# A hybrid decoder trunk: order of products and readings in the expert dispatch and in the last down projection

## Chip, cores and metric

The kernel runs on one NeuronCore of one Trainium2 chip. The metric is device time in microseconds of one launch, from the first to the last instruction of the core with what lies around it. Engines are named as the profile names them: PE (TensorE matmul), PEld (its weight loads), DVE (VectorE), ACT (ScalarE), POOL (GpSimd), and SP, whose queue issues the large DMA transfers.

## What is computed

One layer (`DEPTH = 1`) on 256 tokens and 16 meta tokens of width 2048: a mixer (an mLSTM branch and a sparse attention branch, gated and summed), a LayerNorm, a two-level mixture of experts, a second LayerNorm. The change lies in the mixture of experts and in what feeds the last LayerNorm:

```python
# 32 experts in 4 groups: best group, then the best 2 experts in it
xb = x2[toks]                                   # tokens routed to expert e
gu = xb @ w_gate_up[e]                          # 2048 x 1024 weights
hb = jax.nn.silu(gu[:, :D_FF]) * gu[:, D_FF:]
ys = (hb @ w_down[e]) * ws[:, None]             # 512 x 2048 weights
ffn = segment_sum(ys, row_tok)                  # back to the tokens
h = layer_norm(ALPHA * h + ffn, ln2_g, ln2_b)   # the output, meta rows dropped
```

All 32 experts are computed, each for the (up to 64) tokens that are routed to it, so all weights of w_gate_up and w_down (402 MB) are read from HBM.

## The kernel before

The mixer fills about the first 785 us. Then the experts run in 16 pairs p (two experts of 64 slots each make 128 rows), and every four experts share one dispatch q (q = 0 to 7, before p = 0, 2, 4, ...).

**Dispatch** (`dispatch`, L1017, `bank`, L1029). One-hot matrices `oh` gather the tokens of four experts: `xe[:, k]` (128 features x 256 slots) is a product of the normed activations, split into a high and a low part `uh` and `ul`, with `oh`. A bank is one PSUM tile `pxe` of 512 columns, which holds two values of k: each half is four products (`uh` and `ul` for both blocks of 128 tokens) into one accumulator of 256 columns. Its first half (k even) is read by DVE (L1050), its second half (k odd) by ACT (L1047), both into `xe`. Tiles `pxe` come from a pool of two (`pd`), so a bank's products also wait for the readings of the bank two before it. A dispatch is 8 banks. In dispatch 0 the first two banks run ahead of all, and then chunk n of the first expert (8 products `gu`, which read `xe` of bank n) alternates with bank n + 2. The other dispatches run their 8 banks one behind the other, between two pairs.

**Up and down.** Pair p has 16 chunks (`up_chunk`, L1120), each of which consumes one transfer of 1 MB (`weg`). Between the chunks stand steps of the previous pair's down projection (`down_step`, L1148; 2 transfers `wed` of 1 MB for every four chunks), and the combinations of its pieces (`combine`, L1254). SP issues all transfers in the fixed order of `specs` (L787 to L803): into a slot as soon as its last product on PE has run (`issue`, L809, `used`, L829). Ahead of every fourth chunk the order has two `wed`. All transfers are in this one queue.

**The last down projection** (L1341) has no later chunks to hide in. It runs in five pieces of columns, `LASTP` = 512, 512, 512, 256, 256, each with its own two transfers `wel`. A piece is 16 products `py` on PE, then `gated` (L1271): ACT scales `py` into a high part `yh` (L1277), DVE makes the low part `yl` from `py` and `yh` (L1278); then `combine`: for each of two token blocks PE multiplies `yh` and `yl` by the one-hot matrix into `pc` (pool `pd` again), DVE adds `pc` to `acc` (L1265), takes its statistics by `bn_stats` (L1250), and POOL multiplies it by a LayerNorm row into `fin` (L1251). The final LayerNorm starts with DVE's `bn_aggr` (L1436), which needs the statistics of all pieces.

The order of PE's instructions is that of the program text (`mm` keeps it); on the other engines a scheduler orders the instructions, and each engine runs its own in order.

Of the kernel before, what the change touches and what calls it, by code (L numbers as in the profile page):

```python
# [48 lines left out]
def trunk(ctx, tc, x, meta, ln_emb_g, ln_emb_b, rel_bias, w_in, conv_w, conv_b, b_ig, b_fg,  # L49
# [190 lines left out]
    def fgroup(c0, name, t0=0, raw0=None):  # L240

        n = L - t0
        nk = 8
        pts = [pmt(f"{name}_p{i}") for i in range(2)]
        for kc in range(KD // nk):
            raw = raw0 if raw0 and not kc else load_w(w_in, kc * nk, nk, c0, 256,
                                                      f"{name}_r{kc}")
            if raw0 and kc:
                small_loads()
            for hf in range(2):  # L250
                if raw0:
                    k = kc * nk + hf * 4
                    for k in range(k + 2 if k else 0, min(k + 6, KD)):
                        embed(k)
                wh, wl = split_w(raw[:, hf * 4:hf * 4 + 4], f"{name}_{kc}{hf}")
                k0 = kc * nk + hf * 4
                for kk in range(4):
                    k = k0 + kk
                    for i in range(2):
                        for r in (xhk, xlk):  # L260
                            nc.tensor.matmul(pts[i][:, :n], lhsT=wh[:, kk, i * P:i * P + P],
                                             rhs=r(k, slice(t0, L)), start=k == 0 and r is xhk,
                                             stop=False)
                for kk in range(4):
                    k = k0 + kk
                    for i in range(2):
                        nc.tensor.matmul(pts[i][:, :n], lhsT=wl[:, kk, i * P:i * P + P],
                                         rhs=xhk(k, slice(t0, L)), start=False, stop=k == KD - 1)
                step()
        return pts  # L270
# [349 lines left out]
    for j in range(AH // 2):  # L620
# [8 lines left out]
        pv = fgroup(O_AV + j * 256, f"av{j}")  # L629
# [159 lines left out]
    for p in range(NE // 2):  # L789
        for n in range(16):  # L790
# [5 lines left out]
            e, kc = 2 * p + n // 8, n % 8  # L796
# [206 lines left out]
    def pdt(name):  # L1003
        return pdp.tile([P, 512], F32, name=name, tag="pd")

    def mm(*a, **k):
        late(nc.tensor.matmul(*a, **k))  # L1007
# [4 lines left out]
    def rows_of(k):  # L1012

        o = (k // 2) * 256 + k % 2
        return slice(o, o + 255, 2)

    def dispatch(q):  # L1017


        oh = me.tile([P, 2, 4, C], F32R, name=f"oh{q}", tag="oh", bufs=1)  # L1020
        for b in R2:
            nc.vector.tensor_tensor(
                oh[:, b], iota[:, None, :C].to_broadcast([P, 4, C]),
                rk[:, b, q * 4:q * 4 + 4].unsqueeze(2).to_broadcast([P, 4, C]),
                op=ALU.is_equal)
        xe = me.tile([P, KD, 4 * C], F32, name=f"xe{q}", tag="xe", bufs=1)
        ohf = oh.rearrange("p b e c -> p b (e c)")

        def bank(kc):  # L1029
            if q == 0 and kc % 2 == 0:  # L1030
                for b in R2:
                    sl = slice(kc * 256, kc * 256 + 512)
                    if kc == 0:
                        nc.gpsimd.tensor_tensor(ul[:, b, sl], u[b][:, sl],
                                                uh[:, b, sl].bitcast(F32), op=ALU.subtract)
                    else:
                        late(nc.vector.tensor_tensor(ul[:, b, sl], u[b][:, sl],
                                                     uh[:, b, sl].bitcast(F32), op=ALU.subtract))
            pt = pdt(f"pxe{q}_{kc}")
            for k in (2 * kc, 2 * kc + 1):  # L1040
                pv = pt[:, k % 2 * 256:k % 2 * 256 + 256]
                for i, part in enumerate((uh, ul)):
                    for b in R2:
                        mm(pv, lhsT=part[:, b, rows_of(k)], rhs=ohf[:, b],
                           start=i == 0 and b == 0, stop=i == 1 and b == 1)
                if k % 2:
                    nc.scalar.activation(xe[:, k], pv, AF.Identity, bias=gbp[:, 1, k:k + 1],  # L1047
                                         scale=gbp[:, 0, k:k + 1])
                else:
                    nc.vector.tensor_scalar(xe[:, k], pv, gbp[:, 0, k:k + 1],  # L1050
                                            gbp[:, 1, k:k + 1], op0=ALU.mult, op1=ALU.add)

        for kc in range(2 if q == 0 else 8):
            bank(kc)
        return xe, ohf, bank
# [198 lines left out]
    def combine(nn, c0, n, yh, yl, ohT, first, last):  # L1254

        for b in R2:
            pc = pdt(f"pc{nn}{b}")
            for i, y in enumerate((yh, yl)):
                mm(pc[:, :n], lhsT=ohT[:, b * P:b * P + P], rhs=y[:, :n],
                                 start=i == 0, stop=i == 1)  # L1260
            av = acc[:, b, c0:c0 + n]
            if first:
                nc.vector.tensor_copy(av, pc[:, :n])
            else:
                nc.vector.tensor_tensor(av, pc[:, :n], av, op=ALU.add)  # L1265
            if last:
                finish(b, c0, n)

    def gated_of(p, cur):

        def gated(c0, n, py):  # L1271
            j = p % 2
            gate = cur[1][:, j:j + 1]
            nn = f"{p}_{c0}"
            yh = pre.tile([P, 512], F32R, name=f"yh{nn}", tag="yh", bufs=2)
            yl = pre.tile([P, 512], F32R, name=f"yl{nn}", tag="yl", bufs=2)
            nc.scalar.activation(yh[:, :n], py[:, :n], AF.Copy, scale=gate)  # L1277
            nc.vector.scalar_tensor_tensor(yl[:, :n], py[:, :n], gate, yh[:, :n].bitcast(F32),  # L1278
                                           op0=ALU.mult, op1=ALU.subtract)
            return lambda: combine(nn, c0, n, yh, yl, cur[0][:, j], p == 0, p == LAST)  # L1280
        return gated

    turn = []
    for p in range(NE // 2):
# [4 lines left out]
        for n in range(16):  # L1289
            e, kc = e0 + n // 8, n % 8  # L1290
# [47 lines left out]
    nm5 = me.tile([P, 2, 4, 32], F32, name="nm5", tag="hb", bufs=1)  # L1338
    nc.vector.memset(nm5, 1.0)
    gated = gated_of(LAST, cur)  # L1340
    for c0, n in LASTP:  # L1341
        py = pyp.tile([P, 512], F32, name=f"py{LAST}_{c0}", tag="py")
        for kk in range(4):
            for i in range(2):
                mm(py[i * 64:i * 64 + 64, :n], lhsT=hTs[LAST][:, kk, 64 - i * 64:128 - i * 64],
                                 rhs=live["l", NE - 2 + i, c0][:, kk], start=kk == 0, stop=kk == 3)
        gated(c0, n, py)()

    mp_ctx.close()

# [12 lines left out]
    with tc.If(nmax > C):  # L1363
        with tc.For_i(0, NE, 1) as e:
# [4 lines left out]
            for part in range(2):  # L1369
# [10 lines left out]
                pt = op.tile([P, 512], F32, name="opt" + nn, tag="o0")  # L1380
# [13 lines left out]
                for kc in range(8):  # L1394
# [3 lines left out]
                    for kk in range(2):  # L1398
                        k = kc * 2 + kk
# [6 lines left out]
                pt = op.tile([P, 512], F32, name="opth" + nn, tag="o0")  # L1406
# [3 lines left out]
                for c in range(4):  # L1410
# [3 lines left out]
                    py = op.tile([P, 512], F32, name=f"opy{c}" + nn, tag="og0")  # L1414
# [36 lines left out]
    for u_, (b, n) in enumerate((b, n) for n in range(4) for b in range(2)):  # L1451
        sl = slice(n * 512, n * 512 + 512)
        r = slice(32 * n, 32 * n + 5)
        pt = fp.tile([P, 512], F32, name=f"pt{u_}", tag="pt", bufs=4)
# [38 lines left out]
```

## Time and profile before

| | us |
|---|---|
| median of 3 runs | 1781.91 (1778.19 to 1784.15) |
| profiled execution, its own time | 1773.8 |
| its span | 1772.1 |
| PE busy | 1648.9 (93%) |
| DVE busy | 707.9 (40%) |
| ACT busy | 457.5 (26%) |
| DMA: bytes, mean rate | 537.06 MB, 303 GB/s |

The profile's times are from the start of the span. The busy shares are means over stages with different limits; the table by stage in the section on rows (Rows 1) divides them: there a line is a stretch, with the busy time of PE, PEld, DVE, ACT and POOL and the number of their instructions, then the granted clock of TensorE as a share of 2.4 GHz, the share of time in which the 16 DMA engines worked, and GB/s. In a timeline a row is one instruction or a merged run of equal ones (x8); the time of a PE row includes how long its last result takes to come out, so that rows overlap, and the pace is read from start to start.

### The profile page before, as it was taken

The numbers are of one execution on the slowest core, as the hardware profiler recorded it, in microseconds if no ns is written. First come the engines' busy times: TensorE is split into PE (matmuls) and PEld (weight loads), VectorE is DVE, ScalarE is ACT, GpSimd is POOL, SyncE is SP. The second block draws the span as 40 slices with busy tenths as digits, with TensorE's granted clock in tenths as the row PEclk, the third lists the DMA queues.
The fourth block names the chain that finished last, engine by engine and source line by source line (L and its number), as shares of the span: only waits on it lengthen the run. The fifth ranks groups of instructions, "written<-read, shape, count | busy, mean of one in ns | idle before, by whom it ended". The sixth has DMA issues, their size and how long they took to land. (4 is left out here: it accounts for less than half of the span.)

```text
span 1772.1 us, 20945 instructions
## 1 busy us (share of the span) xinstructions
PE 1648.9 (93%) x8488; PEld 1013.8 (57%) x8488; DVE 707.9 (40%) x1178; ACT 457.5 (26%) x695; POOL 118.2 (7%) x143
## 2 busy tenths in 40 slices
PE   8999999999999999989989899899897988988986
PEld 7988899988787787873343433432433334324332
DVE  7666754454646556452223323421212123202224
ACT  5343444444443443341110100110111001101111
POOL 3002000000302102000100000000000000000002
PEclk9999999999999999999999999999999999999998
DMA  7534454456565578648999999999999999999993
GB/s 221 169 108 132 144 167 143 143 190 229 179 204 178 167 260 301 222 165 303 418 419 420 419 420 419 420 420 419 420 419 419 419 420 420 419 420 419 420 409 118
DMA packets 155941, 537.06 MB, mean 303 GB/s; under 512 B 15724, under 2 KB 64076, under 8 KB 107824
## 3 DMA queue, kind: packets, MB, share of 16 engines
q1 hardware_dynamic: 153552, 530.54, 77.8%
q0 software_dynamic: 2224, 5.12, 1.0%
q8 instruction: 68, 1.11, 0.3%
q14 instruction: 33, 0.27, 0.0%
q10 hardware_dynamic: 64, 0.02, 0.0%
HBM read 533.53 MB, written 2.11 MB: 302 GB/s over the span
## 5 line engine op out<-in xcount | busy, mean ns | idle before, releaser
L1007 PE MATMUL gu<-weg,xe 128*64 128x512 f32 x2032 | 495.5, 610 | 30.5 <-DMA weg<-in_w_gate_up_dram 30.4
L1007 PEld LDWEIGHTS gu<-weg,xe 128*64 128x64 f32 x2032 | 140.2, 139 | 312.0 <-issue 246.9
L1007 PE MATMUL py<-wed,hT 128*64 128x512 f32 x960 | 246.4, 597 | 0.0
L1007 PEld LDWEIGHTS py<-wed,hT 128*64 128x64 f32 x960 | 69.6, 139 | 140.1 <-issue 138.7
L1277 ACT ACTIVATE yh<-py,gsl 128x512 fp32r<-128x512 f32 (+1 forms) x65 | 44.2, 681 | 355.3 <-PE py L1007 340.7
L1278 DVE SCALAR_TENSOR_TENSOR yl<-py,gsl,yh 128x512 fp32r<-128x512 f32 (+1 forms) x65 | 48.0, 738 | 194.4 <-ACT yh L1277 194.4
L1137 DVE TENSOR_TENSOR hb<-gu,hb 64x512 f32<-64x512 f32 x32 | 22.0, 689 | 243.7 <-ACT hb L1136 243.6
L1265 DVE TENSOR_TENSOR acc<-pc,acc 128x512 f32<-128x512 f32 (+1 forms) x122 | 78.9, 678 | 88.1 <-PE pc L1007 87.3
L1136 ACT ACTIVATE hb<-gu 64x512 f32<-64x512 f32 x32 | 18.9, 591 | 341.6 <-PE gu L1007 341.6
L1007 PE MATMUL pxe<-oh,uh 128*128 128x256 f32 x256 | 61.1, 321 | 46.1 <-DVE xe L1050 42.7
L1007 PEld LDWEIGHTS pxe<-oh,uh 128*128 128x128 f32 x256 | 40.9, 199 | 67.8 <-DVE xe L1050 55.8
L1251 POOL TENSOR_TENSOR fin<-acc,fin 128x512 f32<-128x512 f32 (+1 forms) x10 | 10.3, 1053 | 895.0 <-DVE acc L1265 895.0
L1050 DVE TENSOR_SCALAR xe<-pxe,gbp 128x256 f32<-128x256 f32 x64 | 34.7, 543 | 83.8 <-PE pxe L1007 83.8
L1007 PE MATMUL pc<-yh,ohT 128*128 128x512 f32 (+1 forms) x130 | 59.8, 460 | 6.0 <-ACT yh L1277 3.5
L1047 ACT ACTIVATE xe<-pxe,gbp 128x256 f32<-128x256 f32 x64 | 36.0, 563 | 101.1 <-PE pxe L1007 101.1
L1007 PEld LDWEIGHTS pc<-yh,ohT 128*128 128x128 f32 x130 | 24.7, 190 | 54.9 <-issue 23.8
L1007 PE MATMUL pc<-yl,ohT 128*128 128x512 f32 (+1 forms) x130 | 52.4, 403 | 1.1 <-DVE yl L1278 0.9
L1007 PE MATMUL pxe<-oh,ul 128*128 128x256 f32 x256 | 52.4, 287 | 0.0
L1068 DVE TENSOR_SCALAR ohT<-prk,slot 128x512 fp32r<-128x512 f32 x8 | 6.0, 751 | 93.7 <-PE prk L1007 93.7
L1007 PEld LDWEIGHTS pxe<-oh,ul 128*128 128x128 f32 x256 | 41.4, 201 | 0.0
L1007 PEld LDWEIGHTS pc<-yl,ohT 128*128 128x128 f32 x130 | 25.0, 193 | 4.6 <-DVE yl L1278 2.5
L760 POOL TENSOR_TENSOR gms<-gms,gas 128x512 f32<-128x512 f32 x8 | 10.9, 1389 | 224.0 <-DVE gas L759 224.0
(924 smaller groups left out, 3036.7 us busy)
## 6 DMA issues: line engine op xcount, KB each, us to landing
weg<-in_w_gate_up_dram SPq DMA_DIRECT2D x253, 1024.0 KB, 19.9
wed<-in_w_down_dram SPq DMA_DIRECT2D x120, 1024.0 KB, 19.9
gm_r<-in_w_in_dram SPq DMA_DIRECT2D x16, 1024.0 KB, 5.0
ga_r<-in_w_in_dram SPq DMA_DIRECT2D x16, 1024.0 KB, 5.1
wo_r<-in_w_out_dram SPq DMA_DIRECT2D x16, 1024.0 KB, 5.4
qk_r<-in_w_in_dram SPq DMA_DIRECT2D x8, 1024.0 KB, 5.7
mv_r<-in_w_in_dram SPq DMA_DIRECT2D x8, 1024.0 KB, 5.3
aq_r<-in_w_in_dram SPq DMA_DIRECT2D x8, 1024.0 KB, 5.2
```

The costliest lines, as they stand in the source:

```text
L760: nc.gpsimd.tensor_tensor(sg[0][:, b], sg[0][:, b], sg[1][:, b], op=ALU.add)
L1007: late(nc.tensor.matmul(*a, **k))
L1047: nc.scalar.activation(xe[:, k], pv, AF.Identity, bias=gbp[:, 1, k:k + 1], scale=gbp[:, 0, k:k + 1])
L1050: nc.vector.tensor_scalar(xe[:, k], pv, gbp[:, 0, k:k + 1], gbp[:, 1, k:k + 1], op0=ALU.mult, op1=ALU.add)
L1068: nc.vector.tensor_scalar(ohT.rearrange("p a b -> p (a b)"), pr, slot, None, op0=ALU.is_equal)
L1136: nc.scalar.activation(hb[mine], pg_[other], AF.Silu)
L1137: nc.vector.tensor_tensor(hb[mine], pg_[mine], hb[mine], op=ALU.mult)
L1251: nc.gpsimd.tensor_tensor(fin[1 + b][:, c0:c0 + n], acc[:, b, c0:c0 + n], fin[0][:, c0:c0 + n], op=ALU.mult)
L1265: nc.vector.tensor_tensor(av, pc[:, :n], av, op=ALU.add)
L1277: nc.scalar.activation(yh[:, :n], py[:, :n], AF.Copy, scale=gate)
L1278: nc.vector.scalar_tensor_tensor(yl[:, :n], py[:, :n], gate, yh[:, :n].bitcast(F32), op0=ALU.mult, op1=ALU.subtract)
```

## The change

In `bank` the loop over the two halves is split: first the eight products of both halves, then DVE's reading of the first half and ACT's of the second. In the last down projection the combination of a piece is issued behind the products of the next piece; the last piece's combination follows at the end.

```diff
@@ bank (L1041) @@
             for k in (2 * kc, 2 * kc + 1):
                 pv = pt[:, k % 2 * 256:k % 2 * 256 + 256]
                 for i, part in enumerate((uh, ul)):
                     for b in R2:
                         mm(pv, lhsT=part[:, b, rows_of(k)], rhs=ohf[:, b],
                            start=i == 0 and b == 0, stop=i == 1 and b == 1)
+            for k in (2 * kc, 2 * kc + 1):
+                pv = pt[:, k % 2 * 256:k % 2 * 256 + 256]
                 if k % 2:
                     nc.scalar.activation(xe[:, k], pv, AF.Identity, bias=gbp[:, 1, k:k + 1],
                                          scale=gbp[:, 0, k:k + 1])
                 else:
                     nc.vector.tensor_scalar(xe[:, k], pv, gbp[:, 0, k:k + 1],
                                             gbp[:, 1, k:k + 1], op0=ALU.mult, op1=ALU.add)
@@ last down projection (L1340) @@
     gated = gated_of(LAST, cur)
+    then = None
     for c0, n in LASTP:
...
-        gated(c0, n, py)()
+        nxt = gated(c0, n, py)
+        if then:
+            then()
+        then = nxt
+    then()
```

Three places in the built programs show what moves. The first is PE in a bank of dispatch 1 (`pxe_2` is its third bank; what stands in brackets is the engine whose progress an instruction waits for). Before:

```order
L1007 MATMUL pxe_2_7492<-oh_7466,uh 128x256 [waits Activation_49]
L1007 MATMUL pxe_2_7492<-oh_7466,uh 128x256
L1007 MATMUL pxe_2_7492<-oh_7466,ul 128x256 x2
L1007 MATMUL pxe_2_7492<-oh_7466,uh 128x256 [waits DVE_49]
L1007 MATMUL pxe_2_7492<-oh_7466,uh 128x256
L1007 MATMUL pxe_2_7492<-oh_7466,ul 128x256 x2
L1007 MATMUL pxe_3_7503<-oh_7466,uh 128x256 [waits Activation_49]
```

And with the change:

```order
L1007 MATMUL pxe_2_7492<-oh_7466,uh 128x256 [waits Activation_49]
L1007 MATMUL pxe_2_7492<-oh_7466,uh 128x256
L1007 MATMUL pxe_2_7492<-oh_7466,ul 128x256 x2
L1007 MATMUL pxe_2_7492<-oh_7466,uh 128x256 x2
L1007 MATMUL pxe_2_7492<-oh_7466,ul 128x256 x2
L1007 MATMUL pxe_3_7503<-oh_7466,uh 128x256 [waits Activation_49]
```

The products and their order are the same. The wait for DVE ahead of the second half is gone (it is gone from all 64 banks); the wait for ACT ahead of the bank, which guards the reuse of the tile, stays. ACT's reading waits for DVE's in both programs.

The second place is PE between two pieces of the last down projection (`py_0`, `py_512`, `py_1024` are the products of the pieces that begin at these columns, `pc_00` and `pc_01` the combination of the first piece for the two token blocks). Before:

```order
L1007 MATMUL py_0_11275<-wel_0_11115,hT_11229 64x512
L1007 MATMUL py_0_11275<-wel_0_11117,hT_11229 64x512
L1007 MATMUL pc_00_11288<-yh_0_11284,ohT_11142 128x512
L1007 MATMUL pc_00_11288<-yl_0_11285,ohT_11142 128x512
L1007 MATMUL pc_01_11295<-yh_0_11284,ohT_11142 128x512
L1007 MATMUL pc_01_11295<-yl_0_11285,ohT_11142 128x512
L1007 MATMUL py_512_11302<-wel_512_11119,hT_11229 64x512
L1007 MATMUL py_512_11302<-wel_512_11127,hT_11229 64x512
```

And with the change, where the rows ahead are those of the second piece:

```order
L1007 MATMUL py_512_11288<-wel_512_11119,hT_11229 64x512
L1007 MATMUL py_512_11288<-wel_512_11127,hT_11229 64x512
L1007 MATMUL pc_00_11301<-yh_0_11284,ohT_11142 128x512
L1007 MATMUL pc_00_11301<-yl_0_11285,ohT_11142 128x512
L1007 MATMUL pc_01_11308<-yh_0_11284,ohT_11142 128x512
L1007 MATMUL pc_01_11308<-yl_0_11285,ohT_11142 128x512
L1007 MATMUL py_1024_11315<-wel_1024_11135,hT_11229 64x512
L1007 MATMUL py_1024_11315<-wel_1024_11158,hT_11229 64x512
```

The four products of a combination have moved behind the eight pairs of products of the next piece. The last piece's combination stands behind that of the piece before it.

The third place is DVE in the same stretch, from the first piece's `yl` on. Before:

```order
L1278 SCALAR_TENSOR_TENSOR yl_0_11285<-py_0_11275,gsl_11149,yh_0_11284 128x512
L1265 TENSOR_TENSOR acc<-pc_00_11288,acc 128x512
L1265 TENSOR_TENSOR acc<-pc_01_11295,acc 128x512
L1250 BN_STATS st_7031<-acc 128x6 x4
L1278 SCALAR_TENSOR_TENSOR yl_512_11312<-py_512_11302,gsl_11149,yh_512_11311 128x512
L1265 TENSOR_TENSOR acc<-pc_5120_11315,acc 128x512
L1265 TENSOR_TENSOR acc<-pc_5121_11322,acc 128x512
L1250 BN_STATS st_7031<-acc 128x6 x4
```

And with the change:

```order
L1280 SCALAR_TENSOR_TENSOR yl_0_11285<-py_0_11275,gsl_11149,yh_0_11284 128x512
L1267 TENSOR_TENSOR acc<-pc_00_11301,acc 128x512
L1280 SCALAR_TENSOR_TENSOR yl_512_11298<-py_512_11288,gsl_11149,yh_512_11297 128x512
L1252 BN_STATS st_7031<-acc 128x6 x2
L1267 TENSOR_TENSOR acc<-pc_01_11308,acc 128x512
L1252 BN_STATS st_7031<-acc 128x6 x2
L1267 TENSOR_TENSOR acc<-pc_5120_11328,acc 128x512
L1280 SCALAR_TENSOR_TENSOR yl_1024_11325<-py_1024_11315,gsl_11149,yh_1024_11324 128x512
L1252 BN_STATS st_7031<-acc 128x6 x2
L1267 TENSOR_TENSOR acc<-pc_5121_11335,acc 128x512
L1267 TENSOR_TENSOR acc<-pc_10240_11355,acc 128x512
L1252 BN_STATS st_7031<-acc 128x6 x2
```

Before, a piece's `yl`, its two additions and its four statistics stand together. Now a `yl` of the next piece stands between the two additions of a piece, and the statistics are spread in pairs; further on the second addition of the third piece stands behind the fourth piece's `yl` and two pairs of statistics. The number of instructions is the same (5 `yl`, 10 additions, 16 statistics).

On the other engines the order is as before, but for one exchange in dispatch 1: ACT's `yh` of a pair's last piece and DVE's `gr` now stand ahead of the reading of the dispatch's first bank. SP's and POOL's order is unchanged.

## Rows read from the trace of the kernel before

**Rows 1.** Busy time by engine, granted clock, DMA share and GB/s, by stage.
```profile
790.60:799.60 9.00, 7.65 (x24) 4.41 (x24) 2.39 (x5) 6.41 (x14) 0.00 (x0) 0.50 0.00 0
799.60:821.70 22.10, 18.27 (x92) 9.14 (x92) 7.19 (x19) 2.81 (x5) 0.00 (x0) 1.00 0.82 301
...
860.00:1709.00 849.00, 770.59 (x3522) 301.05 (x3518) 200.39 (x340) 95.29 (x155) 0.00 (x0) 0.98 1.01 420
...
1730.00:1757.00 27.00, 20.87 (x100) 8.42 (x100) 13.85 (x31) 3.59 (x6) 10.07 (x10) 1.00 0.25 84
```

**Rows 2.** Timeline of PE, first dispatch: start us, length us, instruction, [idle before, releaser].
```profile
790.60 0.80 PE L1007 MATMUL pxe<-oh,uh 128*128 128x256 f32 x2 [1.19 <-ACT u L948]
791.20 0.63 PE L1007 MATMUL pxe<-oh,ul 128*128 128x256 f32 x2
...
793.56 0.63 PE L1007 MATMUL pxe<-oh,uh 128*128 128x256 f32 x2
793.99 0.63 PE L1007 MATMUL pxe<-oh,ul 128*128 128x256 f32 x2
...
796.40 3.50 PE L1007 MATMUL gu<-weg,xe 128*64 128x512 f32 x8
799.84 0.52 PE L1007 MATMUL pxe<-oh,uh 128*128 128x256 f32 x2
...
801.23 0.51 PE L1007 MATMUL pxe<-oh,uh 128*128 128x256 f32 x2 [0.64 <-DVE xe L1050]
...
801.91 1.94 PE L1007 MATMUL gu<-weg,xe 128*64 128x512 f32 x8
```

**Rows 3.** Timeline of SP's DMA issues, 785 to 835 us.
```profile
830.47 3.76 SPq L823 DMA_DIRECT2D weg<-in_w_gate_up_dram  x3
```

**Rows 4.** The page's costliest groups: the two readings of the banks.
```profile
L1050 DVE TENSOR_SCALAR xe<-pxe,gbp 128x256 f32<-128x256 f32 x64 | 34.7, 543 | 83.8 <-PE pxe L1007 83.8
...
L1047 ACT ACTIVATE xe<-pxe,gbp 128x256 f32<-128x256 f32 x64 | 36.0, 563 | 101.1 <-PE pxe L1007 101.1
```

**Rows 5.** Timeline of PE inside dispatch 7.
```profile
1606.03 0.40 PE L1007 MATMUL pxe<-oh,uh 128*128 128x256 f32 x2
1606.27 0.40 PE L1007 MATMUL pxe<-oh,ul 128*128 128x256 f32 x2
```

**Rows 6.** Timeline of PE: chunks that waited for a weight transfer.
```profile
1212.86 3.49 PE L1007 MATMUL gu<-weg,xe 128*64 128x512 f32 x8 [2.48 <-DMA weg<-in_w_gate_up_dram]
...
1694.77 3.68 PE L1007 MATMUL gu<-weg,xe 128*64 128x512 f32 x8 [4.44 <-DMA weg<-in_w_gate_up_dram]
...
1709.73 1.94 PE L1007 MATMUL gu<-weg,xe 128*64 128x512 f32 x8 [0.51 <-DMA weg<-in_w_gate_up_dram]
```

**Rows 7.** Timeline of PE in the closing stretch.
```profile
1717.61 0.50 PE L1007 MATMUL pc<-yh,ohT 128*128 128x512 f32 x1
...
1718.73 1.94 PE L1007 MATMUL gu<-weg,xe 128*64 128x512 f32 x8
...
1729.90 3.65 PE L1007 MATMUL py<-wel,hT 128*64 128x512 f32 x16
...
1736.02 3.65 PE L1007 MATMUL py<-wel,hT 128*64 128x512 f32 x16
```

**Rows 8.** Timeline of DVE in the closing stretch.
```profile
1734.32 0.75 DVE L1278 SCALAR_TENSOR_TENSOR yl<-py,gsl,yh 128x512 fp32r<-128x512 f32 x1 [5.26 <-ACT yh L1277]
1735.66 1.29 DVE L1265 TENSOR_TENSOR acc<-pc,acc 128x512 f32<-128x512 f32 x2 [0.59 <-PE pc L1007]
1736.87 1.40 DVE L1250 BATCH_NORM_STATS2 st<-acc 128x6 f32<-128x256 f32 x4
...
1754.39 0.48 DVE L1278 SCALAR_TENSOR_TENSOR yl<-py,gsl,yh 128x256 fp32r<-128x256 f32 x1 [1.23 <-ACT yh L1277]
1755.35 0.76 DVE L1265 TENSOR_TENSOR acc<-pc,acc 128x256 f32<-128x256 f32 x2 [0.48 <-PE pc L1007]
1756.02 0.74 DVE L1250 BATCH_NORM_STATS2 st<-acc 128x6 f32<-128x256 f32 x2
```

## Prediction

> **What bounds the kernel now.** I read the table by stage first, then PE's timeline where a stage begins or ends, then who waits. The table shows that after the mixer two different things set the time. From 860 to 1709 us the DMA engines work without a pause (share 1.01, 420 GB/s) [rows 1]: the stream of weights is the bound, and PE's own idle time there costs nothing. But the stream starts late. From 790.6 to 799.6 us it stands still (share 0.00), and up to 821.7 it runs at 0.82 and 301 GB/s [rows 1], because all slots are full and SP issues a transfer only when PE has used one up; the last such start is at 830.47 [rows 3]. So the stretch from 790.6 to 830 is set by PE, and what PE gains there, the whole stream gains. At the other end the transfers run out (share 0.25 of 27 us, so some 6.8 us of work, in 1730 to 1757 [rows 1]), while PE goes on with the five pieces of the last down projection: that stretch is set by the chain PE, ACT, DVE.
>
> **The change, part by part.** *Dispatch 0.* PE's timeline shows its banks [rows 2]. Bank 0 begins at 790.60, the first chunk at 796.40: two banks, 5.80 us at a granted clock of 0.50 [rows 1], which is the 1.2 GHz level. A pair of products there takes 0.43 us (793.56 to 793.99), the first pair 0.60 (790.60 to 791.20). Without the wait for DVE ahead of each second half, 16 products take 0.60 + 7 x 0.43 = 3.61, and with 0.09 for the switch to the chunk 3.70: 2.1 us less, so the first chunk starts at 794.30. It takes 3.44 us (796.40 to 799.84), to 797.74.
>
> Now the clock. It rises to 1.00 at 799.6 [rows 1]. I take it that it rises at the same instant, not at the same instruction, because all that changes for PE until then are two waits of some 0.7 us. The Trainium skill, page "TensorE: Matmul & The Clock Gate", section "What's actually happening", says that the clock is released by a time of activity and not by a number of matmuls; by it the sum is the one taken here, by a release at the same product it would be 0.8 us more, and no row of this trace tells the two apart. Then bank 2 runs at half clock up to there: 1.98 us (0.60 + 3 x 0.43 + 0.09), of which 1.86 lie ahead of 799.6, and chunk 1 starts at 799.66 in place of 801.91 [rows 2], 2.25 us early. At full clock a bank takes 2.07 now (799.84 to 801.91 [rows 2]). A half that follows a wait takes 0.68 with the switch (801.23 to 801.91 [rows 2]), and a pair that follows without one 0.24 [rows 5]; so without the wait a bank takes 0.68 + 2 x 0.24 = 1.16, 0.91 less. Five banks (3 to 7) give 4.55. In sum PE is **6.8 us** ahead at the end of dispatch 0.
>
> What hides the readings that now start later: DVE's takes 0.54 and ACT's 0.56 us [rows 4], one behind the other, and between a bank and the chunk that reads it stand another chunk and another bank, over 2 us. `ul`, which DVE makes ahead of banks 2, 4 and 6, stands on DVE behind a reading that is now later relative to its bank; this is the thinnest cover in this part. Should it fail by half a reading, that costs 3 x 0.27 = 0.8 us; I take 0. Does the lead reach the stream? From 799.6 to 830.47 the engines move 30.9 us x 301 GB/s = 9.3 MB [rows 1, 3], which at 420 GB/s is 22.1 us of work. If it begins 2.1 us earlier, at 797.5, it is through by about 820 to 822 with the last landing, and the next issue, moved from 830.47 by 6.8, comes at 823.7: just enough room. A larger lead would not reach the end in full. Bounds: if only the waits themselves go (8 rows with about 0.64 [rows 2]), 5.1, and 4.3 with `ul` late; if the clock rises with the same work, 2.1 + 6 x 0.91 = 7.6.
>
> *Dispatches 1 to 7* save as much each on PE or a little less (there the reuse of the tile, which waits for DVE's and then ACT's reading, is the next limit: 0.54 + 0.56 and the way there). I cost this at nothing: the stream beside them is saturated [rows 1]. It comes back as longer waits of PE for `weg`.
>
> *The last down projection.* A piece of 512 columns takes 6.12 us on PE (1729.90 to 1736.02 [rows 7]), of which the 16 products with the switch are about 3.5; the rest is PE waiting for `yh` and `yl`. Where nothing is waited for, a combination takes 1.12 (1717.61 to 1718.73 [rows 7]). With the next products in between, PE would start the pieces at 0, 3.45, 8.1, 12.75 and 15.8 us after the first (a piece of 256 columns has half the product time). But then DVE is late next. Its first `yl` comes 4.42 after the piece's start (1734.32 [rows 8]), its first addition waits for PE's combination, and the first addition of the second piece cannot start before PE begins that combination at 11.6 and 0.8 more have passed, 12.4 (0.8 is an estimate from the 0.59 that DVE now waits between `yl` and addition [rows 8] and one product more). From there on DVE hardly idles. What is left in its order: four additions of 512 (4 x 0.645), four of 256 (4 x 0.38), one `yl` of 512 (0.75), two of 256 (2 x 0.48) and 12 statistics (12 x 0.35) [rows 8]: 10.0 us, and some 0.2 of small gaps, so the last statistics end at 22.6 after the first piece's start. Now they end at 1756.02 + 0.74 [rows 8], 26.86 after 1729.90. That is **4.2 us** less, 5.5 if DVE kept up with PE, and 3 if it waits once more for a `pc` tile, of which there are two. POOL's products follow the additions and are done before `bn_aggr` needs POOL. The transfers for these pieces end before PE's present pace needs them; at the new pace the last piece still starts after them.
>
> *Sum:* 6.8 + 4.2 = 11.0 us off the profiled execution's 1773.8, which gives 1762.8. That execution is 8.1 below the median of the runs, 1781.91; the same saving there gives **1770.9**.
>
> **The rivals.** *The waits move to the weights and cost the clock.* After a wait of 4.44 us for `weg`, and after one of 2.48, the eight products of a chunk take 3.68 and 3.49 us; after one of 0.51 they take 1.94 [rows 6]. The change gives PE some 5 us (8 x 0.64) more slack behind each dispatch, so there will be more such waits. In the middle that is free. It counts if the last wait, now 0.51 at 1709.73, grows beyond about 2.5: then one or two of the last chunks run at half clock, which costs 1.6 us each, up to 3: 11 - 3 = 8 us gained, 1774. Against it: the wait of 4.44 one step earlier (1694.77) costs PE enough clock time that the next one stays short, and this alternation should stay. The Trainium skill, page "TensorE: Matmul & The Clock Gate", section "HAM oscillation — how this bites in real kernels", describes just this: a PE that waits for DMA is throttled again and starts its next work cold. By that rule, the trace agrees after 4.44 and 2.48 us, and it speaks against any change that turns short stalls into longer waits.
>
> *Slower, the same mechanism at the end.* If the clock fell at 1709.73 and did not come back before the last piece, the stretch to the last piece's `yl` at 1754.39 [rows 8], 44 us with some 40 of PE work, would run at half pace for its full length and lose up to 20 us; against 11 saved, 9 slower, 1791. A stretch at half clock loses half its length, so this decides from 22 us at half clock on. Against it: after the wait at 1694.77 full pace was back by 1709.73 [rows 6], and behind that nothing waits for a transfer.
>
> *Only the tail.* The lead of dispatch 0 does not reach the end: a clock that rises later eats it, or the stream was not held by PE's slots alone. Then 4.2 us are left, 1777.7, which can't be told from no change. Against it stands the DMA share of 0.00 for 9 us [rows 1].
>
> *Only the dispatch.* DVE's new order, with a `yl` between the additions and statistics ahead of the last additions, holds the tail up: 6.8 us, 1775.1.
>
> *The change doesn't do what it says.* PE's wait would move to the tile's reuse. In dispatch 0 a chunk stands between the banks, so this can matter in dispatches 1 to 7 alone, where it is hidden.
>
> **How the numbers follow.** A measurement of this kernel tells about 0.3% from no change, 5.3 us. Forecast (8 to 13 us): 0.60. Last wait at half clock (8): 0.09. Only the dispatch (6.8): 0.11. Only the tail, or less (0 to 4.2): 0.15. Slower: 0.05. The first three and most of what the fourth borders on are faster by over 0.3%, but 6.8 lies near the bound, so I put faster at 0.77, no difference at 0.18, slower at 0.05. The range goes from the sum of the upper bounds (7.6 + 5.5 = 13.1, 1768.8) less some 3 us for the spread of the runs, 1765.5, to the case of the tail alone with a little spread, 1779.
>
> **What would show it.** In the profile after: no PE row `pxe` that waits for DVE inside a bank; the first chunk near 794.3 and the last chunk behind a bank near 814.8; the full stream some 7 us earlier; more and longer waits of `gu` for `weg` in the middle at the same 420 GB/s; the last one still below 2.5 us; in the tail no `pc` that waits for `yh`, the pieces 3.5 to 4.7 us apart, and 22 to 23 us from the first product to the last statistics. I am wrong if the clock rises well after 799.6, if the stream's end does not move with the dispatch, or if DVE's last statistics end later than 24 us after the first piece.

## The result and the profile after

The changed kernel takes 1767.74 us (median of 4 runs, 1765.61 to 1769.04) against 1781.7 (4 runs, 1778.19 to 1784.15): ratio 0.9921, 95% interval 0.9904 to 0.9938, so 14.0 us less, 11.0 to 17.1 by the interval. A second series gave 0.992 (0.9903 to 0.9938). The forecast was 1770.9: right in sign and within its range, 3 us too high. The gain of 14.0 lies 1 us above the 8 to 13 us of the forecast's main case, and no other case had more; the interval reaches into that case.

The two profiled executions differ by 4.8 us only (1773.8 and 1769.04), because dispatch 0 begins at 790.60 us in the one [rows 2] and at 797.10 in the other, and nothing of the change stands ahead of it. A second profile of the kernel before (below) begins at 797.17; with that one the stages can be set side by side. This table, worked out from the timelines of TensorE and VectorE, is the frame for all that follows. "Dispatch 0" runs from its first product to the chunk behind its last bank, "grid" from there to the first product of the last down, "tail" from there to the end of the last statistics, "rest" from there to the execution's own time.

| execution | dispatch 0 begins | dispatch 0 | grid | tail | rest | own time |
|---|---|---|---|---|---|---|
| before | 790.60 | 31.02 | 908.28 | 26.86 | 17.04 | 1773.80 |
| before, second | 797.17 | 30.49 | 908.88 | 28.55 | 16.99 | 1782.08 |
| after | 797.10 | 21.98 | 908.62 | 23.51 | 17.83 | 1769.04 |
| after, second | 794.15 | 21.98 | 908.90 | 25.05 | 17.96 | 1768.04 |

From "before, second" to "after", which begin at the same time: -8.5 in dispatch 0, -0.3 in the grid, -5.0 in the tail, +0.8 in the rest, -13.0 in sum, about what the medians say.

Busy time by stage, kernel after (columns as in [rows 1]):
```profile
797.10:799.89 2.79, 2.79 (x17) 2.48 (x17) 0.67 (x2) 2.48 (x5) 0.00 (x0) 0.77 0.00 0
799.89:803.94 4.05, 4.05 (x17) 1.79 (x16) 1.75 (x3) 2.62 (x7) 0.00 (x0) 0.74 0.03 6
803.94:819.08 15.14, 15.14 (x82) 7.58 (x81) 6.65 (x18) 2.82 (x5) 0.00 (x0) 1.00 0.95 361
819.08:827.93 8.85, 8.85 (x43) 3.07 (x44) 1.24 (x2) 2.43 (x3) 0.00 (x0) 1.00 1.00 420
860.00:1707.00 847.00, 769.27 (x3510) 299.00 (x3506) 200.46 (x339) 95.24 (x155) 0.00 (x0) 0.97 1.01 420
1727.70:1751.21 23.51, 20.84 (x101) 8.85 (x100) 13.36 (x31) 3.60 (x6) 9.76 (x10) 0.94 0.29 94
```
In dispatch 0 PE is now busy without a gap (15.14 of 15.14 us), and the transfers follow at 0.95 and then 1.00 where they ran at 0.82 [rows 1].

PE's timeline, dispatch 0, kernel after:
```profile
797.10 0.64 PE L1007 MATMUL pxe<-oh,uh 128*128 128x256 f32 x2 [1.16 <-DVE oh L1022]
...
799.89 2.97 PE L1007 MATMUL gu<-weg,xe 128*64 128x512 f32 x8
802.79 0.51 PE L1007 MATMUL pxe<-oh,uh 128*128 128x256 f32 x2
...
803.94 1.94 PE L1007 MATMUL gu<-weg,xe 128*64 128x512 f32 x8
...
806.97 1.94 PE L1007 MATMUL gu<-weg,xe 128*64 128x512 f32 x8
...
819.08 3.65 PE L1007 MATMUL gu<-weg,xe 128*64 128x512 f32 x16
```
No wait stands inside a bank. Bank and chunk take 3.03 us (803.94 to 806.97), where they took 3.94 (801.91 to 805.85 in the profile of before): 0.91 less, as forecast. SP's restart, in the timeline of its issues, follows:
```profile
827.93 5.48 SPq L823 DMA_DIRECT2D weg<-in_w_gate_up_dram  x4
```
That is 30.8 us after the dispatch began, against 39.9 [rows 2, 3]: 9.0 earlier.

The two readings of a bank on the page of the kernel after; what they take and the idle time before them:
```profile
L1052 DVE TENSOR_SCALAR xe<-pxe,gbp 128x256 f32<-128x256 f32 x64 | 34.8, 544 | 44.8 <-PE pxe L1007 42.9
...
L1049 ACT ACTIVATE xe<-pxe,gbp 128x256 f32<-128x256 f32 x64 | 36.0, 564 | 55.8 <-DVE xe L1052 55.7
```
They last as long as before [rows 4], but ACT now waits for DVE's reading and not for products. In a later dispatch that becomes PE's limit, 0.28 us per two banks; PE's timeline in dispatch 2, kernel after:
```profile
998.51 0.52 PE L1007 MATMUL pxe<-oh,uh 128*128 128x256 f32 x2 [0.31 <-DVE acc L1267]
...
1000.99 0.51 PE L1007 MATMUL pxe<-oh,uh 128*128 128x256 f32 x2 [0.28 <-ACT xe L1049]
...
1003.45 0.51 PE L1007 MATMUL pxe<-oh,uh 128*128 128x256 f32 x2 [0.27 <-ACT xe L1049]
```
What PE gains there comes back as waits for weights. PE's waits from 860 to 1760 us, kernel after (us, times, longest):
```profile
PE gu L1007 <- DMA weg<-in_w_gate_up_dram: 58.9, 25, 5.6
PE pxe L1007 <- ACT xe L1049: 6.3, 21, 0.8
```
Before, these were 30.4 us in 14 waits for `weg` and 37.6 us in 56 waits of `pxe` for DVE. The last waits for weights, PE's timeline, kernel after:
```profile
1677.34 1.94 PE L1007 MATMUL gu<-weg,xe 128*64 128x512 f32 x8 [1.33 <-DMA weg<-in_w_gate_up_dram]
...
1692.29 3.14 PE L1007 MATMUL gu<-weg,xe 128*64 128x512 f32 x8 [4.43 <-DMA weg<-in_w_gate_up_dram]
...
1707.26 1.94 PE L1007 MATMUL gu<-weg,xe 128*64 128x512 f32 x8 [1.74 <-DMA weg<-in_w_gate_up_dram]
```
The last wait grew from 0.51 [rows 6] to 1.74 us, and the chunk behind it still ran at the full clock.

The tail, PE's timeline, kernel after:
```profile
1727.70 8.42 PE L1007 MATMUL py<-wel,hT 128*64 128x512 f32 x32
1736.05 0.50 PE L1007 MATMUL pc<-yh,ohT 128*128 128x512 f32 x1
...
1749.06 0.36 PE L1007 MATMUL pc<-yh,ohT 128*128 128x256 f32 x1 [0.96 <-DVE acc L1267]
```
and DVE's in the same stretch:
```profile
1733.46 0.75 DVE L1280 SCALAR_TENSOR_TENSOR yl<-py,gsl,yh 128x512 fp32r<-128x512 f32 x1 [6.89 <-ACT yh L1279]
1736.82 0.69 DVE L1267 TENSOR_TENSOR acc<-pc,acc 128x512 f32<-128x512 f32 x1 [2.60 <-PE pc L1007]
...
1741.54 0.69 DVE L1267 TENSOR_TENSOR acc<-pc,acc 128x512 f32<-128x512 f32 x1 [1.34 <-PE pc L1007]
...
1744.55 0.69 DVE L1267 TENSOR_TENSOR acc<-pc,acc 128x512 f32<-128x512 f32 x1 [0.41 <-PE pc L1007]
...
1750.47 0.74 DVE L1252 BATCH_NORM_STATS2 st<-acc 128x6 f32<-128x256 f32 x2
```
PE no longer waits for `yh` and `yl` [rows 7, 8]; DVE waits for PE early and works without a gap from 1744.55 on, and at the end PE waits for DVE (0.96).

### The profile page after: what moved, and what is told of

Read it like the earlier page. It is cut to its first block, busy times and chain, and to the rows that moved or that the text cites. A ratio compares the mean times of both kernels' runs of the same rounds, so it can differ in the third digit from the quotient of the medians.

```text
span 1767.3 us, 20880 instructions
## 1 busy us (share of the span) xinstructions
PE 1654.4 (94%) x8488; PEld 1018.8 (58%) x8488; DVE 709.4 (40%) x1178; ACT 457.6 (26%) x695; POOL 118.3 (7%) x143
## 5 line engine op out<-in xcount | busy, mean ns | idle before, releaser
L1007 PE MATMUL gu<-weg,xe 128*64 128x512 f32 x2032 | 501.2, 616 | 58.9 <-DMA weg<-in_w_gate_up_dram 58.9
L1007 PE MATMUL py<-wed,hT 128*64 128x512 f32 x960 | 250.3, 606 | 0.0
L1007 PE MATMUL pxe<-oh,uh 128*128 128x256 f32 x256 | 55.8, 299 | 9.6 <-ACT xe L1049 6.3
```

## The experiments

**One part alone.** First the split of the banks without the new tail, and the new tail without the split.

Split alone:
```diff
+            for k in (2 * kc, 2 * kc + 1):
+                pv = pt[:, k % 2 * 256:k % 2 * 256 + 256]
                 if k % 2:
```


> The kernel before with the split bank loop in all dispatches, the last down projection as it was. Theory A (the gain is dispatch 0's lead on PE, handed to the weight stream, plus the shorter tail): 6.8 to 9 us faster than before, the rest of the 14 us belongs to the tail; the tail from first product to last statistics stays at 26.9 us. Rival B (dispatches 1 to 7 are not free, the stream gains there too): 10 us or more. Rival C (nearly all of it is the tail): under 4 us.

Measured: 1770.46 us (6 runs, 1768.25 to 1773.41), ratio 0.9945 (0.9929 to 0.9961) to 1780.72, by the ratio -9.8 us (so all differences of this section, where nothing else is said). That is just above theory A's 6.8 to 9 and just under rival B's 10. In its profile the tail didn't stay at 26.9 us: it took 29.72, because the clock was at half for its first 5.7 us.

Tail alone (the loop over the last pieces, as in the change):
```diff
-        gated(c0, n, py)()
+        nxt = gated(c0, n, py)
+        if then:
+            then()
+        then = nxt
+    then()
```


> The kernel before with the combination of a piece behind the next piece's products, the banks as they were. Theory A: 3.4 to 5.5 us faster, 22 to 23.5 us from the first product of the last down projection to the last statistics (26.9 before). Rival C: 8 us or more. The two parts alone should add up to the whole, 14 us, within the spread.

Measured: 1775.82 us (12 runs, 1770.56 to 1782.15), ratio 0.9976 (0.996 to 0.9991), -4.3 us. In its profile the clock holds in the tail, which takes 22.17 us, 4.7 less than the 26.86 before. The parts add up: 9.8 + 4.3 = 14.1.

**Which dispatch.** The split in dispatch 0 alone (below), and in 1 to 7 alone (the same line with `q > 0`):
```diff
+            for ks in (((2 * kc, 2 * kc + 1),) if q == 0 else ((2 * kc,), (2 * kc + 1,))):
+                for k in ks:
...
```


> The split bank loop in dispatch 0 alone. Theory A: the same as the split in all dispatches, 6.8 to 9 us faster, within 2 us of it. Rival B: clearly less than the split in all, half of it or under.

> The split bank loop in dispatches 1 to 7 alone; each of these dispatches should take PE 9.5 us in place of 15.5. Theory A: no change, within 1.5 us; PE's waits for weights grow by what the dispatches save, 30.4 to about 60 us in sum. Rival B: 3 us or more faster. Rival D (longer waits cost the clock at the end): 1.6 to 3 us slower.

Measured: dispatches 1 to 7 alone 1781.69 (12 runs, 1777.66 to 1783.15), ratio 1.0002 (0.9991 to 1.0012): nothing, as forecast, and PE's waits for `weg` rise from 30.4 to 59.7 us, as expected. Dispatch 0 alone 1775.39 (12 runs, 1766.48 to 1781.62), ratio 0.9974 (0.9954 to 0.9994): -4.6, half of what all dispatches give, as rival B had it. So 1 to 7 are worth nothing alone and about 5 us on top of dispatch 0. By the intervals alone this is close (0.9945 reaches up to 0.9961, 0.9974 down to 0.9954). The spread says more. The five runs with a mean clock of 0.965 to 0.967 took 1779 to 1782 us, the other seven (0.970 to 0.980) 1766 to 1776. The profile (1774.97) has dispatch 0 in 22.68, but the grid in 912.67 us, 4.4 more than before. PE's timeline, dispatch 2, dispatch 0 alone split:
```profile
1000.48 0.51 PE L1007 MATMUL pxe<-oh,uh 128*128 128x256 f32 x2 [0.90 <-DVE xe L1053]
...
1002.34 0.76 PE L1007 MATMUL pxe<-oh,uh 128*128 128x256 f32 x2 [0.64 <-DVE xe L1053]
...
1005.02 0.80 PE L1007 MATMUL pxe<-oh,uh 128*128 128x256 f32 x2 [0.64 <-DVE xe L1053]
...
1021.18 3.68 PE L1007 MATMUL gu<-weg,xe 128*64 128x512 f32 x8
```
Busy time by stretches of 10 us, same kernel:
```profile
1000.00:1010.00 10.00, 7.42 (x32) 6.34 (x32) 2.20 (x5) 2.26 (x4) 0.00 (x0) 0.62 1.01 420
1010.00:1020.00 10.00, 7.64 (x29) 6.53 (x29) 2.03 (x4) 1.84 (x4) 0.00 (x0) 0.50 1.02 419
1020.00:1030.00 10.00, 10.00 (x31) 3.42 (x31) 7.02 (x12) 1.00 (x2) 0.00 (x0) 0.68 0.80 315
1030.00:1040.00 10.00, 10.00 (x48) 3.73 (x48) 1.29 (x2) 0.00 (x0) 0.00 (x0) 1.00 0.88 325
```
SP's issues, same kernel:
```profile
1004.70 2.82 SPq L823 DMA_DIRECT2D wed<-in_w_down_dram  x2
1024.90 11.09 SPq L823 DMA_DIRECT2D weg<-in_w_gate_up_dram  x4
```
The clock fell to 0.50 inside a dispatch in the old order, at 1002.4 us, and stayed there to 1026.3, behind the dispatch's end: a bank takes 2.7 us (1002.34 to 1005.02) instead of 1.86. PE used up no weights meanwhile, SP issued nothing from 1007.5 to 1024.9, and the queue ran dry: 0.80 and 0.88. The Trainium skill, page "TensorE: Matmul & The Clock Gate", section "HAM oscillation — how this bites in real kernels", describes a clock lost to one long wait for DMA; the trace agrees behind the wait of 4.43 us above, and here shows the loss with no wait over 0.90 in the dispatch.

**Is it the clock in the old dispatches, or their length?** Dispatch 0 alone split, with products of the identity that nobody reads in each bank of dispatches 1 to 7. The first attempt put them ahead of a bank:
```diff
+            if q:
+                for n in (128, 64):
+                    mm(fill[:, :n], lhsT=ident, rhs=ident[:, :n], start=True, stop=True)
```


> The split order in dispatch 0 alone (as the run with dispatch 0 alone split, which gained 4.6 us with times 15 us apart), and in dispatches 1 to 7 the old order with 192 columns of identity products, read by nobody, put ahead of each bank's products, so that TensorE has work in the 0.64 to 0.90 us in which it waited for a reading. Theory R (the old dispatches are loose enough that the clock falls to half inside one of them; TensorE then falls behind its weights, the transfers find no free buffer, and part of dispatch 0's lead is lost): with the gaps filled the clock stays up, the weight stream stays at 1.01 of the DMA engines' time, and the whole is 9 to 11 us under the kernel before, with times no more than 6 us apart. Rival S (the old dispatches cost by their length, 15.5 us against 9.5): the length is not changed, so it stays 4 to 6 us under the kernel before and as widely spread.

Measured: 1780.66 (12 runs, 1774.53 to 1785.91), ratio 1.0006 (0.9992 to 1.002), which neither theory said. The place was wrong; PE's timeline, dispatch 2:
```profile
1003.43 0.55 PE L1007 MATMUL fill<-ident 128*128 128x128 f32 x4
1003.80 0.49 PE L1007 MATMUL pxe<-oh,uh 128*128 128x256 f32 x2
...
1005.17 0.51 PE L1007 MATMUL pxe<-oh,uh 128*128 128x256 f32 x2 [0.64 <-DVE xe L1058]
...
1005.75 0.56 PE L1007 MATMUL fill<-ident 128*128 128x128 f32 x4
```
PE waits in the middle of a bank, so the added products lengthen each bank to 2.32 us (1003.43 to 1005.75). The clock is full in all seven dispatches, and still the grid takes 918.31 us, 10 more than before; the stream shows 404 to 415 GB/s in eight of the 17 stretches of 50 us between 860 and 1710, where before has 419 to 420. Longer dispatches can thus starve the stream as well, at the full clock. The second attempt puts them in the middle, where PE waits:
```diff
+                if q and ks[0] % 2:
+                    for n in (128, 64):
+                        mm(fill[:, :n], lhsT=ident, rhs=ident[:, :n], start=True, stop=True)
```


> As the run with dispatch 0 alone split and identity products in dispatches 1 to 7, but these 192 columns stand between the two halves of a bank, where TensorE in fact waits (0.64 to 0.90 us), so that the old dispatches keep their length at the full clock, about 1.9 us a bank. Theory R (the clock inside the old dispatches costs the lead): 9 to 11 us under the kernel before, times no more than 6 us apart, as with all dispatches split. Theory L (their length costs it, at whatever clock: TensorE has 15.5 us in them instead of 9.5, and between the split, the old and the lengthened dispatches the time rises with it): 3 to 6 us under the kernel before, and slices of the weight stream under 1.00 of the DMA engines' time.

Measured: 1770.29 (6 runs, 1766.99 to 1775.26), ratio 0.9946 (0.9929 to 0.9963): the same as with all dispatches split (0.9945), and 5 us below the run with empty gaps, though those two intervals touch (0.9963 and 0.9954). Of its six runs none took more than 1776 us, where five of the other's twelve took 1779 or more. PE's timeline, dispatch 2:
```profile
998.65 0.55 PE L1007 MATMUL fill<-ident 128*128 128x128 f32 x4
999.45 0.51 PE L1007 MATMUL pxe<-oh,uh 128*128 128x256 f32 x2 [0.25 <-DVE xe L1058]
...
1000.52 0.55 PE L1007 MATMUL fill<-ident 128*128 128x128 f32 x4
```
The bank keeps its length (1.87 us, 998.65 to 1000.52), the clock stays up, the grid takes 909.03. So the old dispatches, at their own length and the full clock, cost nothing of the lead; theory R holds against theory L. The times spread over 8 us, 2 more than expected. What stays open is how often the clock falls in an old dispatch, and why it does so more readily behind a split dispatch 0: of the 14 profiles one shows products of dispatches 1 to 7 at half clock, that with dispatch 0 alone split, while the two of before and that of the tail alone, which keep the old order too, show none. But in three profiles with empty gaps the clock fell within 2 us behind a dispatch's last bank, with no wait for weights ahead of it (tail alone at 1019.6 us, the first filling at 1142.2, before at 1018.0), so that the next chunk was slow; PE's timeline, kernel before:
```profile
1017.65 3.33 PE L1007 MATMUL gu<-weg,xe 128*64 128x512 f32 x8
```
With the split order or the gaps filled (63 dispatches in nine profiles) it fell neither in a dispatch nor in the 8 us behind one. So the old order with empty gaps costs the clock now and then in each of the four kernels that have it in these dispatches; what differs is where the fall lands. That it is frequent inside the dispatches behind a split dispatch 0 rests on the five runs with a low mean clock.

**The kernel before again.**

> The kernel before once more, for a second profile. Theory M (the gain is larger than the difference of the two profiled executions because the profiled execution of before was a quick one): this one takes 1778 to 1783 us, and the extra stands where the change does nothing: dispatch 0 begins at 796 to 798 us instead of 790.6, or the weight stream has slices under 1.01. Rival: its stages take what they took in the first profile, to 1 us, and the time is 1773 to 1775 us.

Measured: 1779.07 (8 runs, 1774.34 to 1782.08), the profiled run 1782.08. PE's timeline:
```profile
797.17 0.64 PE L1007 MATMUL pxe<-oh,uh 128*128 128x256 f32 x2 [1.16 <-DVE oh L1022]
...
802.63 3.33 PE L1007 MATMUL gu<-weg,xe 128*64 128x512 f32 x8
...
807.96 1.94 PE L1007 MATMUL gu<-weg,xe 128*64 128x512 f32 x8
...
1736.54 5.35 PE L1007 MATMUL py<-wel,hT 128*64 128x512 f32 x16
```
The first half of theory M holds: dispatch 0 begins 6.6 us later. The second does not, since the grid takes the same to 0.6 us. The other difference is in the tail, 28.55 us: the clock was at half at its first piece, which takes 5.35 us instead of 3.65 [rows 7].

**The kernel after again**, beside the runs that build on it.

> The changed kernel once more, beside the runs that build on it. 12 to 15 us faster than the kernel before, times no more than 6 us apart; dispatch 0 in 22 to 23 us, and between its end and the last but one awaited chunk 873 to 874 us.

Measured: 1767.75 (6 runs, 1762.61 to 1770.89), ratio 0.992 (0.9903 to 0.9938), -13.4 us by the medians; the times are 8.3 apart, not 6. Dispatch 0 takes 21.98 again, and from its end to the last but one awaited chunk it is 873.5 us, as expected.

**What dispatch 0 still loses to the clock.** Three more products of the identity, one ahead of the rank products and two behind them:
```diff
-    keep_warm(11, "warm1")
+    keep_warm(12, "warm1")
...
+    keep_warm(2, "warm2")
     rkf = rk.rearrange("p a b -> p (a b)")
```


> The changed kernel with two more identity products between the rank products and dispatch 0, and one more ahead of the rank products, so that TensorE has work in most of the 1.16 and 0.83 us in which it waits there. Theory A (what dispatch 0 still loses at half clock comes from these two waits): its 22.0 to 22.9 us from the first product to the chunk after the last bank become 20 to 21, and the whole is 1 to 2 us faster than the changed kernel, about 15 to 16 under the kernel before. Rival: the low clock comes from the loose stretch ahead of them (788 to 795 us), or from the first banks themselves, and nothing changes within 1 us; or the added products delay the first bank by up to 0.5 us.

Measured: 1765.86 (6 runs, 1762.26 to 1768.23), ratio 0.9919 (0.99 to 0.9938), -14.4. PE's timeline:
```profile
797.32 0.65 PE L1008 MATMUL pxe<-oh,uh 128*128 128x256 f32 x2 [0.62 <-issue]
...
799.57 1.94 PE L1008 MATMUL gu<-weg,xe 128*64 128x512 f32 x8
```
The first chunk runs at the full clock (1.94 where it took 2.97), and dispatch 0 takes 20.41 instead of 21.98 (20.41 too in the run with both sets of identity products, below): the two waits were the cause of what was left, as theory A has it. In the whole time the 1.6 us can't be told apart from the kernel after.

**Is the tail bound by VectorE?** The combination behind half of the next piece's products:
```diff
+            if kk == 1 and then:
+                then()
+        then = gated(c0, n, py)
...
```


> The changed kernel with the combination of a piece of the last down put behind 8 of the next piece's 16 products, not behind all 16. Theory A (the tail is bound by VectorE, which after its first step still waited 2.60, 1.34 and 0.41 us for the combining products): the first combining products come 1.7 us earlier, VectorE's waits shrink by 2 to 3 us in sum, and so does the tail: 2 to 3 us faster than the changed kernel, 16 to 17 under the kernel before. Rival (the tail is bound by TensorE, which waits for the two readings of the piece when its combination comes earlier): waits of 0.3 to 1.1 us for the readings come back at each of four pieces, and it is 0 to 3 us slower than the changed kernel.

Measured: 1767.72 (6 runs, 1763.71 to 1772.1), ratio 0.9934 (0.9913 to 0.9956): no gain. DVE's timeline:
```profile
1734.79 0.75 DVE L1280 SCALAR_TENSOR_TENSOR yl<-py,gsl,yh 128x512 fp32r<-128x512 f32 x1 [0.46 <-ACT yh L1279]
1736.44 1.29 DVE L1267 TENSOR_TENSOR acc<-pc,acc 128x512 f32<-128x512 f32 x2 [0.90 <-PE pc L1007]
...
1739.50 0.75 DVE L1280 SCALAR_TENSOR_TENSOR yl<-py,gsl,yh 128x512 fp32r<-128x512 f32 x1 [0.46 <-ACT yh L1279]
```
DVE starts sooner, but waits twice in each piece of 512. From the first `yl` (1730.08) to the last statistics (1748.48) it takes 18.4 us, against 17.8 in the kernel after (1733.46 to 1751.21). The tail took 25.60 us with its first 24 products at a low clock (8.15 us). So VectorE isn't the bound alone, and theory A fell. That PE and DVE need about the same time, so that moving the hand-over only moves the wait, is the likeliest reading; no run shows it apart.

**Can the clock be held at the tail?** Identity products of 64 columns behind the last combining products and the scale's products:
```diff
+            filler(64)
             av = acc[:, b, c0:c0 + n]
...
+            pt = bcast_rows(2, n, f"pg2{n}")
+            filler(64)
```


> The changed kernel with 64 columns of identity products, read by nobody, behind each of the last combining products ahead of the last down and behind the four products of the final scale, where TensorE has gaps of about 0.3 us. Theory C (the clock falls to half at the first piece of the last down because that stretch is loose; it did so in the three profiles with the split order in dispatches 1 to 7 and in none of the three without): the first 32 products take 7.0 us where they took 8.4, the final norm loses less, and the whole is 1 to 3 us faster than the changed kernel, 15 to 17 under the kernel before. Rival: the clock falls there for something earlier, or VectorE hides it, and it stays within 1 us of the changed kernel.

Measured: 1767.72 (6 runs, 1763.49 to 1770.25), ratio 0.9936 (0.9919 to 0.9954), -11.4, no better than the kernel after. In its profile the first 32 products take 7.09 us, and the tail 22.20. With this and the products ahead of dispatch 0 together:

> The changed kernel with both sets of identity products: three ahead of dispatch 0 and 64 columns behind each of the last combining and scale products. If each gives what its profile shows (dispatch 0 in 20.4 us instead of 22.0 to 22.9; the last down's first 32 products in 7.1 us instead of 8.4), the whole is 1.5 to 3 us faster than the changed kernel, which runs beside it. Rival: what is won in dispatch 0 is waited for later, at a weight, and what is won at the end is spent on the added products: within 1 us of the changed kernel.

Measured: 1766.8 (6 runs, 1763.76 to 1769.4), ratio 0.9917 (0.9901 to 0.9933), 0.95 us under the kernel after beside it, which is no difference that can be told. Its PE timeline shows why the end gives nothing:
```profile
1724.64 8.74 PE L1008 MATMUL py<-wel,hT 128*64 128x512 f32 x32
```
With the same products in place the clock was down all the same, and the tail took 23.86. Theory C fell: the products don't hold the clock there, and the second profile of before lost it without the split. No version here beats the changed kernel by more than can be told. The filled gaps of dispatches 1 to 7 with the new tail were not run.

## Why the prediction was right, and where it was not

*Dispatch 0's lead (6.8 us)* is right in kind and too small; the same-time pair of profiles has 8.5 (30.49 to 21.98). The five banks at the full clock gave 0.91 each, as worked out. The step that failed is "I take it that it rises at the same instant". By the granted clock in slices of 1 us, it is full again 9.0 us (before) and 8.3 us (before, second) after the first product, and 4.9 us (after, twice); with the split alone, which began at 790.81, 5.7. Between profiles that begin alike it came back 3.3 to 3.4 us sooner, at half pace worth 1.7: 6.8 + 1.7 = 8.5. In all 14 profiles it came back 8.1 to 9.5 us after the first product where dispatch 0 has the old order (four), 4.9 to 6.0 where it is split (eight), and it didn't fall in dispatch 0 where three more identity products stand ahead (two).

Term by term, by the same-time pair: the first two banks gave 2.67 us (5.46 to 2.79; 2.1 in the sum), the first chunk with bank 2 1.28 (5.33 to 4.05; 0.15 in the sum), the other five banks 4.56 (4.55 in the sum). In that pair the first two banks began at the full clock and lost it 1.5 us on; in the profile that the prediction read, they ran at half from the start.

The Trainium skill, page "TensorE: Matmul & The Clock Gate", section "What's actually happening", was read as giving the same instant; the runs show that the waits inside the banks had put it off. The bound "if the clock rises with the same work, 7.6" was nearer, but too low too.

*"A larger lead would not reach the end in full"* fell as well: 8.5 us arrived, with the grid at 908.6 against 908.9.

*Dispatches 1 to 7 at nothing* is right for that part alone (1.0002), for the reason given: the stream is saturated. It is wrong beside dispatch 0's lead, which is kept only where PE doesn't fall too far behind in them; there they are worth some 5 us (9.8 against 4.6). No rival of the prediction had this.

*The last down (4.2 us, 22.6 after the first product)* is right: 22.17 where the clock held, -4.3 us with that part alone. The step "DVE is late next" is half right. DVE does end the stretch without gaps, but the half-way hand-over showed PE to be as near a limit. The forecast left out that the clock can be down at the first piece (1.3 us for the first 32 products, 8.42 against 7.09), which happens with and without the change: in seven of the eight profiles with the split in dispatches 1 to 7, and in two of the six without. Whether the split makes it likelier isn't shown.

*The final part* was not costed, and takes 0.6 to 1.7 us more (17.8 to 18.7 us against 17.0 to 17.2) in the eight profiles with the split in dispatches 1 to 7 and in none of the six without. In all eight DVE is idle for 0.66 to 0.67 us ahead of `bn_aggr`, against 0.34 to 0.35 in the six, and for 0.47 to 0.83 ahead of its first conversion behind it, where the six have no gap. What these gaps wait for no trace shows, and no run tried it.

*The rivals.* The last wait came to 1.74 us, below the 2.5 from which it would count, so "waits at half clock" and "slower" didn't come; the mechanism stood one step earlier (4.43), where it always was. The 2.5 is no sharp bound: over the 14 profiles the shortest wait for `weg` with a slow chunk behind it was 2.23 us, the longest with a chunk at full pace 3.92. The price of "slower" was too low as a sum: at half pace 40 us of PE work take 40 us more, not 20. "Only the dispatch" and "only the tail" fell, since both parts came through alone (-9.8 and -4.3) and together. The wait at the tile's reuse is there in dispatches 1 to 7 (0.28 us), small.

## What to carry to other kernels

Time that is won on an engine beside a saturated stream of transfers is worth nothing by itself, but it can keep that engine from falling so far behind that the stream runs dry. So ask of such a saving not only what it gives, but what it protects, and test the parts together as well as alone. A product order that left TensorE with a wait in each short step cost twice here, by the waits and by the clock that they put off or let fall. Taking out the waits gave both back; filling them exactly where they stand gave back the clock, which was all that the later dispatches needed. Before a gain is read from two profiles, set them side by side by stage: an earlier stage may start 6 us apart by chance.

## What the runs showed that was not expected

The start of dispatch 0 falls between 790.6 and 797.7 us over 14 profiles, in kernels that are the same up to there but for three identity products in two of them; that is half of the change's effect. The clock fell inside a dispatch in which no wait was longer than 0.90 us, and stayed at half for 23.9 us, beyond the dispatch's end, while the waits of 0.64 us a bank went on. With the waits in the banks at 0.25 to 0.28 us (the change, or the filled gaps) no profile shows it, though single longer ones are left there, up to 0.57 us (filled) and 0.83 (split, in dispatch 1). And the transfers in the queue lasted through holds of 10.7 us by PE (the longest wait of SP's queue for `gu` in the profile of before), but not through those of 12.7 (the lengthened dispatches) and 15.2 (dispatch 0 alone split).
